# A two-block kernel with a planned instruction order: more places for side work beside the input projections, and an earlier start of four modulation blocks

## The chip, the cores and the metric

The kernel runs on one core of a Trainium2 chip. The metric is the device time of one execution in microseconds; lower is better. The engines are named as the profile names them: PE (matrix multiply, with PEld for its weight loads), DVE (vector), ACT (activation), POOL (GpSimd) and SP (which here only issues DMAs).

## What is computed

The program takes a row matrix `x` of 1024 x 1024 through two blocks, all in float32. What matters of the reference:

```python
# first block
h = rms_norm(x, norm_w)
proj = einsum('bsd,de->bse', h, w_in)            # 1024 -> 6160 columns
gq, gk, gv, glr, hq, hf, hi, xq, gate = split(proj)
# 4 GLA heads and 4 HGRN heads: S_t = diag(g_t) S_{t-1} + k_t v_t^T, o_t = S_t^T q_t
# 4 cross-attention heads over a memory of 256 rows
mixed = concatenate([gla_o, hgrn_o, xo]) * silu(gate)
x = rms_norm(x + einsum('bse,ed->bsd', mixed, w_out), final_norm_w)
# second block
mod = silu(c) @ w_mod + b_mod                    # 6 x 1024: shift, scale, gate, twice
h = modulate(rms_norm_2(x, norm1_g), sh1, s1)
u = h @ w_pw1 + b_pw1; u = a * sigmoid(gate)
u = silu(layer_norm(dwconv(u, w_dw) + b_dw))     # width 31 inside rows of 64
x = x + g1 * (u @ w_pw2 + b_pw2)
x = x + g2 * (square(relu(modulate(rms_norm_2(x, norm2_g), sh2, s2) @ w1)) @ w2)
out = rms_norm_2(x, final_g)
```

## The kernel before, in words

**Products.** Every large product is done as three: each operand is split into a rounded high part and a remainder (`whi`, `wlo` for weights; `hTh`, `hTl` or `acth`, `actl` for activations), and `mm3` (line 444) issues high x high, high x low and low x high into one PSUM tile. Weights arrive by DMA in a tile `wst`; `Weights.plan` (line 278) then lists six pieces of work for it: a cast on ACT into half of `whi`, two subtractions into `wlo` on POOL or DVE, and the same for the other half.

**Main line.** The 1024 rows are worked in two halves of 512. Each half has eight units: four GLA heads (G), two pairs of HGRN heads (H) and two pairs of cross-attention heads (X), in the sequence of the table `ORDER`. Each unit has two to four weight tasks `("in", unit, key)`, the input projections: `in_groups` (line 513) runs them on PE into the PSUM tiles `ps_d`. A group of `cm` (line 495) is 24 matmuls of 512 columns, one of `tm` (line 502) 24 matmuls of 256 or 272 columns. When two units are finished, two output tasks (`out_groups`, line 576) multiply the mixed heads (`mixh`, `mixl`) by `w_out`, eight groups of 12 matmuls of 512 columns. After the second half come `pw1_groups` (line 1100) and `pw2_groups` (line 1202) of the convolution module, which use `tm` too, and then the hidden layer, which the change doesn't touch.

**Side work.** What lies between the projections (factors of the recurrence, scores, masks, states, norms, the modulation) is cut into `Step`s in nine lanes. A step of the recurrence is, for two chunks of 128 rows: `scores` (PE, then COPY_PREDICATED on DVE that puts masked pieces into a tile `at`), `turn` (a transposed key), and `output`, whose first matmul reads `at`. A modulation block (`modulation_steps(cb)`, line 969) loads four tiles `wm` and accumulates them on DVE into `macc`.

**What sets the order.** The kernel has a clock of its own at build time: class `Model` adds up estimated costs per engine, and `M.now` is its time on PE. At each `yield` of a projection group two things happen in the loop at the end of `block_kernel`:

```python
for dt in task.go(hi, lo):
    here += dt
    W.tick(min(1.0, (2.0 if task.key[:2] == ("pw2", 1) else 1.3) * here / task.est))
    service(kind=task.key[0])
```

`W.tick` emits as many of the six weight pieces as the share of the task that is done, times 1.3; `here` grows by 2.6 for each yield and `task.est` is 10.4 for these tasks. `service` emits every step whose inputs are ready by the clock; a step of ordinary rank also needs `room`: DVE's estimated queue must end within the first number of `LIMITS` after `M.now`, ACT's within the second. Each engine then runs its instructions in the order in which they were emitted. `pick` decides which task is staged next: output tasks go ahead of the main line once their two units are finished by the clock. `MODS` says after which unit's gate projection which modulation block may begin; the lane `mod` runs them one after another and then the filter of the convolution.

Of the kernel before, what the change touches and what calls it, by code (L numbers as in the profile page):

```python
# [386 lines left out]
def block_kernel(ctx, tc, x, mem, w_in, w_up, w_kv, w_out, w_mod, w_pw1, w_pw2, w_dw, w_1, w_2,  # L387
# [56 lines left out]
    def mm3(o, pairs, first=True, last=True, more=False):  # L444


        n = len(pairs)
        kw = {"skip_group_check": True} if more else {}
        for i, ((sh, sl), (mh, ml)) in enumerate(pairs):
            PE.matmul(o, sh, mh, start=first and i == 0, stop=False, **kw)  # L450
            PE.matmul(o, sh, ml, start=False, stop=False, **kw)
            PE.matmul(o, sl, mh, start=False, stop=last and i == n - 1, **kw)
# [42 lines left out]
    def cm(p, act, hi, lo, w, c):  # L495

        pairs = [((hi[:, k * w + c:k * w + c + P], lo[:, k * w + c:k * w + c + P]), act.both(k)) for k in range(KT)]
        mm3(p, pairs[:KT // 2], last=False)
        yield TH
        mm3(p, pairs[KT // 2:], first=False)  # L500

    def tm(act, i, hi, lo, w, n):

        p = pt("d")
        c = slice(i * P, (i + 1) * P)
        mm3(p[:, :n], [(act.both(k, c), (hi[:, k * w:k * w + n], lo[:, k * w:k * w + n])) for k in range(KT)])
        return p

    hT = {}
# [3 lines left out]
    def in_groups(t, unit, key, u):  # L513
        kind, h = unit

        def go(hi, lo):
            act = hT[t]
            if key in ("qk", "qf0", "qf1"):
                j = 1 if key == "qf1" else 0
                q = u[f"q{j}"] = s4([P, NT, 192], name="q")  # L520
                p = pt("d")
                yield from cm(p, act, hi, lo, 256, 0)
                A.mul(q[:, :, :P], p.rearrange("p (c t) -> p c t", c=NT), QS if kind == "G" else 1.0)
                yield TH
                k = u[f"k{j}"] = s2([P, T], name="k")
                p = pt("d")
                yield from cm(p, act, hi, lo, 256, P)
                if kind == "G":
                    A.copy(k, p)
                else:  # L530
                    a = u[f"a{j}"] = s2([P, T], name="a")
                    hh = 2 * h + j
                    A.activation(a, p, AF.Sigmoid)
                    A.activation(k, p, AF.Sigmoid, scale=-1.0)
                    V.tensor_scalar(a, a, lbt[:, 4 + hh:5 + hh], lbt[:, 8 + hh:9 + hh], op0=ALU.mult, op1=ALU.add)
                    V.tensor_scalar(k, k, lbt[:, 4 + hh:5 + hh], None, op0=ALU.mult)
                yield TH
            elif key == "v":
                n = 272 if unit == ("G", 3) else 256
                v = u["v"] = s4([P, NT, 256], name="v")  # L540
                g = small(16 * NT, "glr", 1).rearrange("p (i c) -> p i c", i=NT) if n > 256 else None
                for i in range(NT):
                    p = tm(act, i, hi, lo, n, n)
                    if t == 0 and unit == units[0][1] and i < 2:
                        turn0(i + 2)
                    A.copy(v[:, i, :], p[:, :256])
                    if n > 256:
                        V.tensor_copy(g[:, i, :], p[:, 256:272])
                    yield TT
                if n > 256:  # L550
                    gt = glrT[t] = s2([16, T], name="glrT")
                    p = pt("m")
                    for i in range(NT):
                        PE.transpose(p[:16, i * P:(i + 1) * P], g[:, i, :], ident)
                    V.tensor_copy(gt, p[:16, :])
                    mark(("glr", t), gt)
            elif key == "g":
                g = u["gate"] = s4([P, 2, T], name="gate")
                for b in range(2):
                    p = pt("d")  # L560
                    yield from cm(p, act, hi, lo, 256, b * P)
                    A.activation(g[:, b, :], p, AF.Silu)
                    yield TH
            else:
                u["qh"] = s4([P, 2, T], F32R, name="xqh")
                u["ql"] = s4([P, 2, T], F32R, name="xql")
                for b in range(2):
                    p = pt("d")
                    yield from cm(p, act, hi, lo, 256, b * P)
                    A.mul(u["qh"][:, b, :], p, QS)  # L570
                    V.scalar_tensor_tensor(u["ql"][:, b, :], p, QS, u["qh"][:, b, :].bitcast(F32),
                                           op0=ALU.mult, op1=ALU.subtract)
                    yield TH
        return go
# [525 lines left out]
    def pw1_groups(h, cb, part):  # L1100
        def go(hi, lo):
            act = acts[h]
            if part == 0:
                if cb == 0:
                    ys[h] = [s4([P, D], name="y") for _ in range(NT)]
                if (h, cb) == (0, 0):
                    biases(0, 0)
                conv["a", h, cb] = s4([P, NT, 256], name="pa")
            elif (h, cb) != (1, 3):
                biases(*((h, cb + 1) if cb < 3 else (1, 0)))  # L1110
            ba, av = conv["b", h, cb], conv["a", h, cb]
            for i in range(NT):
                p = tm(act, i, hi, lo, 256, 256)
                if part == 0:
                    V.tensor_tensor(av[:, i, :], p[:, :256], ba[:, 0, :], op=ALU.add)
                else:
                    g = s2([P, 2, 256], name="pg")
                    V.tensor_tensor(g[:, 0, :], p[:, :256], ba[:, 1, :], op=ALU.add)
                    A.activation(g[:, 0, :], g[:, 0, :], AF.Sigmoid)
                    V.tensor_tensor(g[:, 1, :], av[:, i, :], g[:, 0, :], op=ALU.mult)  # L1120
                    us = s2([P, 2, 256], F32R, name="us")
                    A.copy(us[:, 0, :], g[:, 1, :])
                    rest(us[:, 1, :], g[:, 1, :], us[:, 0, :].bitcast(F32))
                    later([us], 1, lambda i=i, us=us: conv_fwd(h, cb, i, us))
                yield TT
        return go
# [75 lines left out]
    def pw2_groups(h, nb):  # L1202
        def go(hi, lo):
# [3 lines left out]
            for i in range(NT):  # L1207
                if (h, nb, i) in ((1, 2, 0), (1, 3, 0)):
                    load_w1(nb - 2)
                    done["w1" if nb == 2 else "w1b"] = M.time(raw[nb - 2]) + 2.0  # L1210
                p = tm(acts["v", h], i, hi, lo, 256, 256)
                z = s2([P, 256], name="yg")
                V.tensor_tensor(z, p[:, :256], mods[2][:, c], op=ALU.mult)
                xt = px[h][i]
# [805 lines left out]
GAIN = 0.3  # L2020
FAST = ('kv', 'w1', 'out', 'in', 'pw1', 'pw2', 'w2')
URGENT = (7, 15, 30)
MODS = ((1, 0), (1, 1), (2, 2), (3, 3), (4, 6), (5, 7), (10, 8), (11, 10), (12, 11), (13, 9))
LIMITS = {'in': (3.0, 4.0), '': (3.0, 4.0)}
HOLD = [('in', 6), ('in', 7), ('kv', 0), ('in', 15)]
ORDER = ([('G', 3), ('G', 0), ('G', 2), ('H', 0), ('G', 1), ('H', 1), ('X', 0), ('X', 1)], [('G', 3), ('G', 0), ('G', 1), ('H', 0), ('X', 1), ('H', 1), ('X', 0), ('G', 2)])
N4 = 32
# [63 lines left out]
```

## Time and profile before

| | us |
|---|---|
| median of 3 runs | 2037.58 |
| lowest and highest | 2037.0, 2043.21 |
| the profiled execution | 2028.93 |
| its span, first to last instruction | 2026.8 |
| PE busy | 1945.7 |
| DVE busy | 1512.6 |
| ACT busy | 915.5 |
| POOL busy | 829.7 |

Read it so: the profiled execution is one execution of its own, 8.65 us under the median of the runs; it lies 2.13 us around its span. PE has work in flight in 96% of the span. Since matmuls overlap, an idle stretch of PE shows only where nothing at all is in flight. In the page's forty slices the granted clock of PE is at full speed but for a few, and DMA rises to 70 to 90% only in the last third, the hidden layer.

### The profile page before, as it was taken

The page shows a single profiled execution, that of the slowest core. Times are in us where ns is not written, and L with a number is a line of the kernel's source. Part 1 is how long each engine was busy: PE and PEld are TensorE (multiplying, and loading weights), DVE is VectorE, ACT ScalarE, POOL GpSimd, SP SyncE. Part 2 cuts the span into 40 slices and gives each one's busy share as a digit, 9 for nine tenths or more (in the row PEclk, how much of TensorE's full clock was granted, in tenths as well). Part 3 has the DMA queues.
Part 4 walks back from the last instruction along what each step waited for, and adds up shares of the span by engine and source line. Part 5 has one row for each costly group of instructions (what it writes and reads, how often), then busy time and mean ns, then how long its engine had stood idle before and what let it go on. Part 6 is the DMA issues. An engine that isn't in the chain of part 4 may idle for free.

```text
span 2026.8 us, 29614 instructions
## 1 busy us (share of the span) xinstructions
PE 1945.7 (96%) x10892; PEld 1699.7 (84%) x10892; DVE 1512.6 (75%) x2593; ACT 915.5 (45%) x1790; POOL 829.7 (41%) x752
## 2 busy tenths in 40 slices
PE   8999999999999999998999999999999998899998
PEld 6888898888888888887799999997878886688786
DVE  5688869775677876777757666978888878777876
ACT  6433333455443334344234334235777766443333
POOL 3443443443444432444454343540000003978872
PEclk9999999999999999998999999999999999999999
DMA  5223323241232332322433233241699889877765
GB/s 199 83 104 146 125 105 125 89 162 43 94 145 90 118 124 96 125 84 96 150 122 100 79 98 105 85 151 56 194 299 272 244 262 303 277 271 268 272 248 203
DMA packets 177634, 315.01 MB, mean 155 GB/s; under 512 B 9762, under 2 KB 129442, under 8 KB 163794
## 3 DMA queue, kind: packets, MB, share of 16 engines
q1 hardware_dynamic: 175186, 309.33, 45.3%
q10 hardware_dynamic: 2304, 3.80, 0.5%
q8 instruction: 85, 1.39, 0.3%
q14 instruction: 59, 0.48, 0.1%
HBM read 241.78 MB, written 71.31 MB: 154 GB/s over the span
## 4 chain that ended last, share of the span: by engine, by line
PE 77%; DVE 11%; DMA 4%; ACT 4%; issue 2%; POOL 1%; SPq 0%; DVEq 0%; POOLq 0%; ACTq 0%
PE ps_d L244 50%; PE ps_s L244 20%; PE ps_m L244 7%; DVE macc L244 2%; DMA sl<-so 2%; DVE at L244 2%; DVE zt L244 1%; DVE tw L244 1%; DMA sh<-so 1%; DVE so L244 1%; ACT hc L244 1%; ACT whi L244 1%; POOL tm L244 1%; DVE acc L244 1%; DMA wlo<-sl 0%
## 5 line engine op out<-in xcount | busy, mean ns | idle before, releaser
L244 POOL TENSOR_TENSOR wlo<-wst,whi 128x512 fp32r<-128x512 f32 (+1 forms) x240 | 344.8, 1453 | 376.8 <-ACT whi L244 363.8
L244 PE MATMUL ps_d<-hTh,whi 128*128 128x512 f32 x576 | 232.0, 403 | 0.0
L244 PE MATMUL ps_d<-whi,acth 128*128 128x256 f32 x768 | 221.6, 289 | 7.3 <-DVE yg L244 3.8
L244 ACT CAST whi<-wst 128x1024 fp32r<-128x1024 f32 (+1 forms) x182 | 189.0, 1049 | 81.8 <-PE ps_d L244 72.7
L244 PE MATMUL ps_d<-hTh,wlo 128*128 128x512 f32 x576 | 225.0, 391 | 0.0
L244 PE MATMUL ps_d<-hTl,whi 128*128 128x512 f32 x576 | 224.5, 390 | 0.0
L244 POOL TENSOR_TENSOR wst<-wst,g 128x512 f32<-128x512 f32 x64 | 93.4, 1477 | 316.3 <-DMA g<-g2d 290.9
L244 PE MATMUL ps_d<-whi,actl 128*128 128x256 f32 x768 | 219.9, 286 | 2.1 <-POOL actl L244 1.4
L244 PE MATMUL ps_d<-wlo,acth 128*128 128x256 f32 x768 | 219.3, 285 | 2.3 <-DVE wlo L244 2.3
L244 PE MATMUL ps_s<-tm,whi 128*128 128x512 f32 x620 | 191.8, 391 | 6.1 <-ACT ps_s L244 3.4
L244 PE MATMUL ps_s<-hm,tw 128*128 128x512 f32 x768 | 180.9, 390 | 6.0 <-ACT hc L244 4.6
L244 PEld LDWEIGHTS ps_s<-hm,tw 128*128 128x128 f32 x768 | 143.6, 188 | 37.6 <-ACT hc L244 5.8
L244 PEld LDWEIGHTS ps_d<-whi,acth 128*128 128x128 f32 x768 | 149.2, 194 | 8.3 <-DVE yg L244 4.0
L244 DVE TENSOR_TENSOR wlo<-wst,whi 128x512 fp32r<-128x512 f32 (+1 forms) x128 | 116.7, 922 | 51.6 <-ACT whi L244 50.8
L244 PEld LDWEIGHTS ps_d<-whi,actl 128*128 128x128 f32 x768 | 149.3, 194 | 3.1 <-POOL actl L244 1.9
L244 PEld LDWEIGHTS ps_d<-wlo,acth 128*128 128x128 f32 x768 | 149.3, 194 | 2.8 <-DVE wlo L244 2.5
L244 DVE COPY_PREDICATED at<-msk,ps_s 128x128 f32<-128x128 uint8 (+1 forms) x352 | 117.3, 337 | 41.8 <-PE ps_s L244 27.0
L244 PEld LDWEIGHTS ps_s<-tm,whi 128*128 128x128 f32 x620 | 115.6, 188 | 33.0 <-ACT ps_s L244 5.2
L244 PEld LDWEIGHTS ps_d<-hTh,whi 128*128 128x128 f32 x576 | 108.5, 188 | 23.1 <-issue 2.5
L244 PEld LDWEIGHTS ps_d<-hTh,wlo 128*128 128x128 f32 x576 | 108.1, 188 | 23.4
L244 PEld LDWEIGHTS ps_d<-hTl,whi 128*128 128x128 f32 x576 | 108.5, 188 | 21.0 <-issue 0.2
L244 PE MATMUL ps_s<-tm,wlo 128*128 128x512 f32 x310 | 121.0, 390 | 2.7 <-DMA wlo<-sl 2.7
(289 smaller groups left out, 4977.0 us busy)
## 6 DMA issues: line engine op xcount, KB each, us to landing
wst<-in_w_in_dram SPq DMA_DIRECT2D x46, 1024.0 KB, 4.8
wst<-in_w_dram SPq DMA_DIRECT2D x32, 1024.0 KB, 6.5
sh<-so SPq DMA_DIRECT2D x112, 256.0 KB, 4.3
sl<-so SPq DMA_DIRECT2D x112, 256.0 KB, 4.0
whi<-sh SPq DMA_DIRECT2D x31, 896.0 KB, 4.7
wlo<-sl SPq DMA_DIRECT2D x31, 896.0 KB, 7.3
wm<-in_w_mod_dram SPq DMA_DIRECT2D x48, 512.0 KB, 6.4
wst<-in_w_pw_dram SPq DMA_DIRECT2D x24, 1024.0 KB, 5.0
```

The source lines that it names most:

```text
L244: r = f(*args, **kw)
```

## The change

Three edits. `cm` yields after every two of its eight k-tiles and not after four (three points inside a group and one behind it, before one and one), and `tm` yields once in its middle, where it had no point inside. `MODS` lets the modulation blocks 8, 10, 11 and 9 begin after units 9, 9, 10 and 11, before after 10, 11, 12 and 13 (units are counted from 0, eight to a half). `LIMITS` for the input projections is 4.0 and 5.0, before 3.0 and 4.0.

```diff
     def cm(p, act, hi, lo, w, c):
 
         pairs = [((hi[:, k * w + c:k * w + c + P], lo[:, k * w + c:k * w + c + P]), act.both(k)) for k in range(KT)]
-        mm3(p, pairs[:KT // 2], last=False)
-        yield TH
-        mm3(p, pairs[KT // 2:], first=False)
+        for k in range(0, KT, 2):
+            mm3(p, pairs[k:k + 2], first=k == 0, last=k + 2 == KT)
+            if k + 2 < KT:
+                yield TH
 
     def tm(act, i, hi, lo, w, n):
 
         p = pt("d")
         c = slice(i * P, (i + 1) * P)
-        mm3(p[:, :n], [(act.both(k, c), (hi[:, k * w:k * w + n], lo[:, k * w:k * w + n])) for k in range(KT)])
+        pairs = [(act.both(k, c), (hi[:, k * w:k * w + n], lo[:, k * w:k * w + n])) for k in range(KT)]
+        mm3(p[:, :n], pairs[:KT // 2], last=False)
+        yield TH
+        mm3(p[:, :n], pairs[KT // 2:], first=False)
         return p
...
-                    p = tm(act, i, hi, lo, n, n)
+                    p = yield from tm(act, i, hi, lo, n, n)
...
-MODS = ((1, 0), (1, 1), (2, 2), (3, 3), (4, 6), (5, 7), (10, 8), (11, 10), (12, 11), (13, 9))
-LIMITS = {'in': (3.0, 4.0), '': (3.0, 4.0)}
+MODS = ((1, 0), (1, 1), (2, 2), (3, 3), (4, 6), (5, 7), (9, 8), (9, 10), (10, 11), (11, 9))
+LIMITS = {'in': (4.0, 5.0), '': (3.0, 4.0)}
```

The same `yield from` stands in `pw1_groups` and `pw2_groups`. The number 2.6 that a yield reports (`TH`, `TT`) is as before. No matmul is added or removed: both programs have the same ones, in another order.

**Place 1: SP's queue at the end of the second half.** `wst` are weight loads (`in_w_in` input, `in_w_out` output, `in_w_pw` convolution), `wm` the modulation's, `dft` and `wdw` the filter's, `xn` the rows with which the convolution begins. Before:

```order
L244 DMA wm<-in_w_mod_dram 128x1024 x4
L244 DMA wst<-in_w_in_dram 128x2048 x3
L244 DMA wst<-in_w_pw_dram 128x2048
L244 DMA dft<-in_consts_dram 128x640
L244 DMA wdw<-in_w_dw_dram 31x1024
L244 DMA wst<-in_w_out_dram 128x2x512 x2
L244 DMA xn<-xd_0_71 128x1024
```

Now:

```order
L244 DMA wm<-in_w_mod_dram 128x1024 x4
L244 DMA wst<-in_w_in_dram 128x2048 x4
L244 DMA wst<-in_w_out_dram 128x2x512 x4
L244 DMA dft<-in_consts_dram 128x640
L244 DMA wdw<-in_w_dw_dram 31x1024
L244 DMA wst<-in_w_in_dram 128x2048 x5
L244 DMA wst<-in_w_out_dram 128x2x512 x4
L244 DMA xn<-xd_0_71 128x1024
```

The filter's loads stand some five tasks earlier, and the last pair of output tasks that was staged behind the first convolution weights (`in_w_pw`) is staged ahead of them.

**Place 2: PE at the same seam**, between the last input projection and the first convolution product (`ps_d<-whi,acth`). `ps_s<-q,k` and `ps_s<-Q,K` are scores of the last unit, `ps_s<-ident,xn` and `ps_m<-ident,prob` transposes. Before, without anything left out:

```order
L244 MATMUL ps_m<-wdw,dft 128x512 x2
L244 MATMUL ps_s<-q,k 128x192 x2
L244 MATMUL ps_s<-Q_8564,K_8548 128x192 x2
L244 MATMUL ps_s<-Q_8574,K 128x192 x2
L244 MATMUL ps_s<-Q_8584,K 128x192 x2
L244 MATMUL ps_m<-ident,K 128x128 x2
L244 MATMUL ps_s<-q,k 128x192 x2
L244 MATMUL ps_s<-Q_8564,K_8548 128x192 x2
L244 MATMUL ps_s<-ident,xn 128x128 x12
L244 MATMUL ps_m<-ident,prob 128x128 x4
L244 MATMUL ps_s<-ident,xn 128x128 x16
L244 MATMUL ps_m<-ident,prob 128x128 x4
```

Now, a piece of the same stretch:

```order
L244 MATMUL ps_d<-whi,mixl 128x512
L244 MATMUL ps_s<-Q_8638,K 128x192 x2
L244 MATMUL ps_s<-Q_8648,K 128x192 x2
L244 MATMUL ps_m<-ident,K 128x128 x2
L244 MATMUL ps_s<-q,k 128x192 x2
L244 MATMUL ps_s<-Q_8628,K_8612 128x192 x2
L244 MATMUL ps_s<-ident,xn 128x128 x8
L244 MATMUL ps_d<-whi,mixh 128x512
L244 MATMUL ps_d<-wlo,mixh 128x512
```

The eight output groups of units 12 and 13 (`mixh`, `mixl`, 12 matmuls each) now stand one by one between the scores, transposes and outputs of this stretch; before they stood behind the first convolution task.

**Place 3: PE beside a cm group of the first half**, unit 3, first head (H). `at_122` and `at_123` are the two tiles of masked scores. Before:

```order
L244 MATMUL ps_m<-v,at_122 128x128
L244 MATMUL ps_m<-stH_127,q_2087 128x128
L244 MATMUL ps_m<-v,kT 128x128
L244 MATMUL ps_m<-ident,K 128x128 x2
L244 MATMUL ps_d<-hTh,whi 128x512
L244 MATMUL ps_d<-hTl,whi 128x512
L244 MATMUL ps_d<-hTh,wlo 128x512
L244 MATMUL ps_d<-hTh,whi 128x512
L244 MATMUL ps_d<-hTl,whi 128x512
L244 MATMUL ps_d<-hTh,wlo 128x512
L244 MATMUL ps_d<-hTh,whi 128x512
L244 MATMUL ps_d<-hTl,whi 128x512
```

Now:

```order
L244 MATMUL ps_m<-v,at_122 128x128
L244 MATMUL ps_m<-stH_127,q_1918 128x128
L244 MATMUL ps_m<-v,kT 128x128
L244 MATMUL ps_m<-ident,K 128x128 x2
L244 MATMUL ps_d<-hTh,whi 128x512
L244 MATMUL ps_d<-hTl,whi 128x512
L244 MATMUL ps_d<-hTh,wlo 128x512
L244 MATMUL ps_d<-hTh,whi 128x512
L244 MATMUL ps_d<-hTl,whi 128x512
L244 MATMUL ps_d<-hTh,wlo 128x512
L244 MATMUL ps_m<-v,at_123 128x128
L244 MATMUL ps_m<-stH_127,q_1918 128x128
```

Six projection matmuls stand between the two outputs, before twelve (the piece ends after eight of them).

## Rows read from the trace of the kernel before

**Rows 1.** The page: busy us, share and instructions of each engine; the chain's shares.

```profile
PE 1945.7 (96%) x10892; PEld 1699.7 (84%) x10892; DVE 1512.6 (75%) x2593; ACT 915.5 (45%) x1790; POOL 829.7 (41%) x752
PE 77%; DVE 11%; DMA 4%; ACT 4%; issue 2%; POOL 1%; SPq 0%; DVEq 0%; POOLq 0%; ACTq 0%
```

**Rows 2.** Windows: length, busy us of PE, PEld, DVE, ACT, POOL; clock; DMA.

```profile
50.00:430.00 380.00, 372.01 (x2063) 326.62 (x2062) 298.04 (x575) 146.20 (x291) 165.65 (x152) 1.00 0.33 117
770.00:800.00 30.00, 26.18 (x179) 24.70 (x178) 17.41 (x42) 11.37 (x37) 3.83 (x3) 0.90 0.43 140
935.00:985.00 50.00, 37.46 (x189) 30.99 (x188) 41.10 (x79) 19.05 (x43) 23.02 (x24) 0.83 0.49 155
985.00:1250.00 265.00, 262.68 (x2018) 254.34 (x2017) 167.40 (x273) 101.36 (x160) 115.91 (x110) 1.00 0.28 93
1250.00:1420.00 170.00, 158.99 (x1119) 148.84 (x1119) 138.47 (x217) 68.96 (x108) 66.58 (x62) 0.96 0.29 106
1420.00:2026.00 606.00, 579.23 (x2528) 472.30 (x2526) 478.56 (x692) 338.35 (x625) 235.64 (x184) 1.00 0.80 260
```

**Rows 3.** Chain in order of time: start us, us, what; 512 columns, then 256.

```profile
98.25 2.77 PE ps_d L244 x12
1049.19 2.88 PE ps_d L244 x24
```

**Rows 4.** Timeline of PE at the seam: start us, us, instruction, idle time before it.

```profile
955.87 0.66 PE L244 MATMUL ps_s<-ident,xn 128*128 128x128 f32 x4 [1.15 <-DVE zt L244]
960.97 0.41 PE L244 MATMUL ps_d<-whi,acth 128*128 128x256 f32 x1
967.27 0.39 PE L244 MATMUL ps_d<-whi,acth 128*128 128x256 f32 x1 [1.65 <-ACT acth L244]
974.57 0.28 PE L244 MATMUL ps_d<-whi,acth 128*128 128x256 f32 x1
```

**Rows 5.** Groups of DVE by form: xcount, busy us, mean ns, idle before.

```profile
L244 DVE COPY_PREDICATED at<-msk,ps_s 128x128 f32<-128x128 uint8 x320 | 104.6, 327 | 32.4 <-PE ps_s L244 17.8 <-PE ps_m L244 0.5
L244 DVE TENSOR_TENSOR xl<-ps_d,xl 128x512 f32<-128x512 f32 x64 | 43.8, 685 | 42.3 <-PE ps_d L244 42.0
L244 DVE TENSOR_SCALAR zt<-ps_s,m1s,m1b 128x512 f32<-128x512 f32 x16 | 12.4, 801 | 0.0
```

**Rows 6.** Timelines of DVE and of PE, 785 to 796.

```profile
791.31 1.54 DVE L244 SCALAR_TENSOR_TENSOR macc<-wm,scv,macc 128x512 f32<-128x512 f32 x2 [4.38 <-DMA wm<-in_w_mod_dram]
792.77 2.01 DVE L244 COPY_PREDICATED at<-msk,ps_s 128x128 f32<-128x128 uint8 x6
...
794.92 0.77 PE L244 MATMUL ps_m<-v,at 128*128 128x128 f32 x2 [2.90 <-DVE at L244]
```

**Rows 7.** Waits of PE: us in total, times, longest.

```profile
PE ps_m L244 <- DVE at L244: 11.1, 10, 2.9
PE ps_s L244 <- DVE at L244: 5.1, 9, 1.3
```

**Rows 8.** Timeline of PE in the convolution stage.

```profile
1109.83 0.39 PE L244 MATMUL ps_d<-wlo,acth 128*128 128x256 f32 x1 [2.32 <-DVE wlo L244]
1260.76 0.39 PE L244 MATMUL ps_d<-whi,acth 128*128 128x256 f32 x1 [1.89 <-DVE acth L244]
```

**Rows 9.** Timeline of ACT at the start.

```profile
17.08 2.17 ACT L244 ACTIVATE hTh<-ps_s,pv 128x128 fp32r<-128x128 f32 x8 [2.00 <-PE ps_s L244]
19.34 1.12 ACT L244 CAST whi<-wst 128x1024 fp32r<-128x1024 f32 x1
```

**Rows 10.** Timelines of DVE and POOL, 930 to 936: one form of DVE, alone and beside POOL.

```profile
930.35 0.43 DVE L244 TENSOR_TENSOR Q<-Q,tree 128x256 f32<-128x256 f32 x1
932.84 0.75 DVE L244 TENSOR_TENSOR Q<-q,a 128x256 f32<-128x256 f32 x1
930.70 4.91 POOL L244 TENSOR_TENSOR K<-K,tree 128x256 f32<-128x256 f32 x6
```

More of the change, by code (lines that the diff above doesn't have):

```diff
@@ L1112, in go @@
             for i in range(NT):
-                p = tm(act, i, hi, lo, 256, 256)
+                p = yield from tm(act, i, hi, lo, 256, 256)
                 if part == 0:
@@ L1210, in go @@
                     done["w1" if nb == 2 else "w1b"] = M.time(raw[nb - 2]) + 2.0
-                p = tm(acts["v", h], i, hi, lo, 256, 256)
+                p = yield from tm(acts["v", h], i, hi, lo, 256, 256)
                 z = s2([P, 256], name="yg")
```

## The prediction

> **What bounds the kernel now.** I read the page first. PE is busy in 96% of the span and the chain of waits lies on it for 77%; DVE has 11% of the chain and DMA 4% [rows 1]. So the time is PE's stream, plus what PE waits, plus what it loses at a low clock. The stream cannot shrink: both programs have the same matmuls. The windows then tell where something else than the stream is paid for [rows 2]: 50 to 430, plain projections beside the recurrence, has 7.99 us of PE idle in 380; 985 to 1250, in the convolution, 2.32 in 265; but 935 to 985, the seam between the last input projection and the convolution, has 12.54 idle in 50 and a granted clock of 0.83. The seam's timeline shows both losses [rows 4]: PE waits 1.15 for `zt` on DVE and 1.65 for `acth` on ACT, and between them one matmul of 256 columns takes 0.41, which later takes 0.28: it ran at 1.2 GHz after the idle stretches, and at 2.4 GHz again by 974.57. A second such place, 770 to 800, has 3.82 idle and a clock of 0.90. There DVE waited 4.38 for a `wm` load, the six mask copies behind it took 2.01, and PE stood 2.90 for `at` [rows 6]. The rest are short waits, PE for `at` and for other work of DVE: 11.1 us at ten places and 5.1 at nine [rows 7].
>
> The prices of a gap on PE are twelve matmuls of 512 columns in 2.77 us and 24 of 256 columns in 2.88 [rows 3]: 0.231 and 0.120 each, whatever was issued between them, so cutting a group in two costs nothing by itself.
>
> **The change part by part.**
>
> *The seam.* More points let steps finish earlier by the planner's clock, so the last two output tasks are staged ahead of the convolution, and their eight groups stand between the scores, transposes and outputs (place 2). That is 8 x 2.77 = 22.2 us of PE work put where PE idled. They left the stage 985 to 1250, which is 99% busy and simply becomes shorter. What is to be had is the idle, 12.54, and the low clock, (1 - 0.83) x 37.46 = 6.4: 18.9 in all; the other end is nothing. DVE must keep up: its 41.10 busy us [rows 2] and eight `xl` additions at 0.685 [rows 5] make 46.6, against 37.46 - 6.4 + 22.2 = 53.3 of PE. It fits, with 6.7 to spare. What stays is the two waits at the seam, for `zt` (each 0.801 on DVE [rows 5]) and for `acth` [rows 4], since the convolution still begins with them, 2.8, and the 2% idle of the stage 50 to 430 on 53 us, 1.1. Taken: -18.9 + 3.9 = **-15.0**.
>
> *The modulation.* Blocks 8, 10, 11 and 9 start up to two units sooner, the `wm` loads and the additions into `macc` with them; the filter's loads and its product follow sooner as well. SP gets these loads ahead of weight loads that they stood behind; output weights now stand ahead of convolution weights (place 1). The place at 770 to 800 loses its modulation. Its worth is 3.82 idle and (1 - 0.90) x 26.18 = 2.6 of clock, 6.4; if the blocks meet a late `wm` at their new place and again hold copies up, it costs as much again. DVE's work is the same amount. I take the idle alone, **-4**, between -6.4 and +6.4, because it took a coincidence of a late load and copies right behind it [rows 6] that shows at one block.
>
> *Weight pieces.* `here` grows by 2.6 at each of twice as many yields, so the six pieces of a weight are emitted in the first 40% of a task, not the first 80%. `wlo` comes sooner: the wait of 2.32 for it at 1109.83 [rows 8] can go, **-2** (0 to -2.3). Some ten remainders go from POOL to DVE; at twice the 0.685 of a 512-wide addition [rows 5] that is an estimated 14 us, spread over the run, of a DVE that is busy in 75%. On ACT, 45% busy [rows 1], casts come closer together. Nothing for these; their cover is the idle of both engines, and the third rival is what it costs if that fails.
>
> *Half the spacing, one more microsecond of DVE queue.* This is the edit with a possible loss. Between two steps that follow each other there were twelve projections, 2.77 us, and now often six, 1.39 (place 3). An `output` waits for six copies at 0.327 [rows 5], 2.0 us, in which 2.77 is cover enough and 1.39 is not. But a step is emitted only when its inputs are ready by the clock, so halving offers points and does not force them. Counted over the 32 pairs of scores and first `output` of the second half, 13 had under 3 us of projections between them, and 14 have it now. One pair at the mean wait of 1.1 (11.1 over ten [rows 7]) and as much for the longer queue: **+2**. The ends are -8 (the idle of 50 to 430 goes altogether) and +16 (0.5 us on each of the 32).
>
> *Convolution.* `tm` with a point inside does the same in `pw1` and `pw2`. Between the last transposes of the normalised rows and the product that needs them there were 48 matmuls of 256, now 36: 5.8 against 4.3 us of cover. PE already waited 1.89 for that `acth` [rows 8], so what cover loses the wait gains: **+1.4** (0 to +1.4). From the last `pw2` task on, PE's order is the same, so the 606 us of 1420 to 2026 stay.
>
> *The start.* A CAST of the second weight now precedes a group of turned rows on ACT. It takes 1.12 us, in a place where ACT stood idle for 2.00 [rows 9]. **0** (to +1.1, were that idle gone).
>
> Sum: -15.0 - 4 - 2 + 2 + 1.4 = **-17.6**. The profiled execution took 2028.93 (2026.8 of span and 2.13 around it), so it would take 2011.3. The median of the runs lies 8.65 above that execution; I put the same on top: **2020**.
>
> **The rivals.**
>
> *The waits only move.* The output groups need mixed heads that the same steps produce, and DVE has just 6.7 us to spare in the seam. If they wait for DVE in their turn, the idle of 12.54 comes back among them and only the clock is won. For it: DVE is already what PE waits for there [rows 4]. Against: these groups are 22 us of work that is ready when the two units are. -17.6 + 12.5 = -5.1: 2032 (2028 to 2039).
>
> *Copies under pressure: slower.* If half the spacing, with DVE's limit at 4 and not 3 us, puts the copies of each pair 1 us later than its `output` wants them, 32 pairs pay 32 us. In place of my +2 the sum is -19.6 + 32 = +12.4: 2050 (2040 to 2060). It cancels the gains from 0.61 us a pair. For it: 1.39 us is less than the six copies take. Against: of the whole 2027 us only ten such waits are seen, with a longest of 2.9, though 13 of 32 pairs had under 3 us already.
>
> *DVE and POOL collide.* An operation of DVE on 128x256 takes 0.43 by itself and 0.75 with POOL at work [rows 10]. Pieces of weights that come in a bunch put more of POOL's work, 166 of 380 us, beside DVE's copies. If a tenth more of DVE's 298 us falls beside POOL, that is 30 x 0.74 = 22 us more DVE work out of its 82 idle; PE's 7.99 of idle, grown as that slack shrinks (82/60), becomes 10.9, so +2.9 for each 380 us, and +6.8 over some 880 us of projections: 2027. The Trainium skill, "Perfetto Trace Analysis", section Optimizing Scalar/DVE Operations, says that GpSimd and DVE share a read port of SBUF, so that moving work between the two might not help. By that rule the ten remainders that go to DVE are no loss, and the bunching is; the two durations agree with it, without showing the cause.
>
> *The clock falls in shorter batches.* The stage 50 to 430 had twelve-matmul batches between steps and a clock of 1.00; 1250 to 1420, where more steps lie between, 0.96 [rows 2]. If halved batches brought 0.96 to the projections, 880 us x 0.979 busy x 0.04 = +34: 2054. Against: what stands between the batches is matmuls too, and idle, not switching, went ahead of the low clock at the seam [rows 4]. The Trainium skill, same page, section Matmul Optimizations, says that the engine scales its power by utilisation and wants matmuls back to back in batches. By that rule shorter batches would speak against this change; the seam agrees that idle costs clock, and no row shows a short batch without idle losing any.
>
> *Not as said.* The order's seam could prove empty because the output weights land late (SP has other loads ahead): 2038.
>
> **How the numbers follow.** Chances: forecast 0.53, waits that move 0.20, copies 0.12, collision 0.10, batches 0.03, not as said 0.02. The forecast's own range is 2010 (both places return in full, the other terms at their best ends without the -8) to 2031 (the seam gives half and 770 to 800 nothing). A measurement of this kernel tells about 0.3%, 6.1 us, from no change: faster is under 2031.5, slower over 2043.7. Faster: 0.53, nearly all of the collision (0.09) and 0.06 of the moved waits, 0.68. Slower: batches 0.03 and 0.09 of the copies, 0.12. The rest, 0.20, is no change. The range 2008 to 2041 leaves out most of the copies, the batches, and a few hundredths below.
>
> **What would show it.** Right: the stretch before the convolution has PE over 92% busy at a clock near 1.00, with output groups among scores; no stretch like 770 to 800; PE's waits for `at` near 11 to 15 us; the hidden layer as long as before. Wrong: PE's waits for `at` at 25 us or more, at many places; a clock under 1.00 beside projections with PE busy; mask copies whose mean grows over 327 ns; or output groups that each wait for `mixh` or `mixl`.

## The result: 1.5% faster, by more than was forecast

| | before | after |
|---|---|---|
| median, us | 2039.93 (4 runs, 2037.0 to 2043.21) | 2009.52 (4 runs, 2008.76 to 2012.59) |
| profiled execution, us | 2028.93 | 2009.97 |
| its span, us | 2026.8 | 2007.7 |
| its granted clock, mean | 0.989 | 0.990 |

The ratio is 0.9853, with an interval of 0.9832 to 0.9875. The forecast was 2020 (2008 to 2041): the result lies at the fast end of that range, and just outside the 2010 to 2031 that I gave for the case that my mechanism holds. The two profiled executions differ by 18.96 us, where I had forecast 17.6; the medians differ by 30, and by 28 in a later comparison (e9). The section on why the prediction came out takes both numbers apart.

The page of the changed kernel, engines and chain, answering to [rows 1]:

```profile
PE 1940.9 (97%) x10892; PEld 1693.9 (84%) x10892; DVE 1512.9 (75%) x2603; ACT 918.9 (46%) x1791; POOL 815.1 (41%) x742
PE 79%; DVE 11%; issue 3%; DMA 3%; POOL 2%; ACT 2%; SPq 0%; DVEq 0%; POOLq 0%; ACTq 0%
```

The work is the same and so is each engine's share. PE idles for 2007.7 - 1940.9 = 66.8 us, before 81.1, and its busy time is 4.8 shorter at the same 10892 matmuls. The mean clock of 0.990 for 0.989 makes some 2 us of these 4.8 (0.001 of 1940.9, and three digits are all it is given in); the rest isn't located. The windows show where PE idles. Columns as in [rows 2]; the last one is 606 us of hidden layer, shifted to where it lies now:

```profile
50.00:430.00 380.00, 372.87 (x2053) 326.43 (x2052) 298.86 (x584) 144.90 (x290) 158.31 (x148) 1.00 0.32 114
430.00:770.00 340.00, 333.75 (x1850) 289.85 (x1849) 247.78 (x463) 142.29 (x315) 144.06 (x137) 0.98 0.34 118
770.00:800.00 30.00, 30.00 (x211) 28.51 (x211) 18.52 (x43) 14.66 (x41) 7.51 (x8) 1.00 0.23 71
800.00:935.00 135.00, 134.75 (x749) 116.57 (x748) 94.56 (x201) 61.00 (x160) 59.21 (x65) 1.00 0.24 82
935.00:985.00 50.00, 46.87 (x270) 40.64 (x269) 41.61 (x72) 17.22 (x35) 23.07 (x21) 1.00 0.34 115
985.00:1250.00 265.00, 258.91 (x2046) 252.96 (x2046) 179.59 (x288) 108.55 (x170) 116.53 (x109) 0.99 0.32 112
1250.00:1400.00 150.00, 141.91 (x1004) 131.80 (x1003) 127.20 (x204) 62.42 (x96) 50.88 (x50) 0.99 0.29 104
1401.00:2007.00 606.00, 580.22 (x2509) 472.64 (x2508) 475.35 (x686) 337.77 (x624) 235.20 (x184) 0.99 0.79 259
```

Two windows of the kernel before that [rows 2] doesn't have:

```profile
430.00:770.00 340.00, 335.51 (x1861) 292.22 (x1861) 243.80 (x454) 145.69 (x322) 143.00 (x135) 0.99 0.30 103
800.00:935.00 135.00, 132.61 (x733) 115.15 (x732) 101.14 (x202) 54.52 (x145) 57.93 (x60) 1.00 0.28 98
```

The seam, 935 to 985, has 3.13 us of PE idle where it had 12.54, and a clock of 1.00 where it had 0.83. At 770 to 800 there is no idle at all. From 800 to 935 the idle fell from 2.39 to 0.25, and between 1250 and the hidden layer from 11.01 to 8.09, at a clock of 0.99 and not 0.96. Two windows have become worse: 430 to 770 idles 6.25 (before 4.49, and the clock is 0.98 for 0.99), and the convolution, 985 to 1250, 6.09 (before 2.32, and 0.99 for 1.00). The hidden layer idles 25.78 against 26.77, at 0.99 for 1.00. The windows are stretches of time: after the seam the same work lies some 19 us earlier than before.

PE in the seam, where the last output groups (`mixh`) now stand between scores and transposes:

```profile
945.15 0.89 PE L244 MATMUL ps_s<-q,k 128*128 128x192 f32 x4 [1.57 <-DVE at L244]
948.18 0.33 PE L244 MATMUL ps_s<-ident,xn 128*128 128x128 f32 x1 [0.33 <-DVE xn L244]
949.45 0.48 PE L244 MATMUL ps_d<-whi,mixh 128*128 128x512 f32 x1
952.30 0.59 PE L244 MATMUL ps_m<-v,at 128*128 128x256 f32 x2
```

The longest wait that remains is one of 1.57 for `at`; four more, for `at`, `xn` and `wlo`, are of 0.31 to 0.53. The `output` at 952.30 waits for nothing: twelve matmuls of an output group have run ahead of it. The waits for `zt` and for `acth` that opened the convolution [rows 4] are gone.

Of PE's waits (us in total, times, longest), those that bear on the argument:

```profile
PE ps_d L244 <- DVE pa L244: 5.4, 2, 3.7
PE ps_m L244 <- DVE at L244: 4.8, 6, 1.1
PE ps_d L244 <- DVE yg L244: 4.2, 1, 4.2
PE ps_d L244 <- ACT mixh L244: 3.2, 1, 3.2
PE ps_s L244 <- DVE at L244: 2.4, 3, 1.6
```

The waits for `at` were 11.1 and 5.1 [rows 7] and are 4.8 and 2.4, at nine places and not nineteen. Two kinds of wait are new: `pa`, in the convolution, and `mixh`, early in the second half. The rows of these two, DVE first, then PE:

```profile
1046.94 1.23 DVE L244 TENSOR_TENSOR conv_b_pw<-conv_b_pw,gate_bc 128x1024 f32<-128x1024 f32 x1 [4.79 <-DMA conv_b_pw<-in_rows_dram]
```

```profile
540.84 0.80 PE L244 MATMUL ps_d<-whi,mixh 128*128 128x512 f32 x1 [3.24 <-ACT mixh L244]
1048.55 0.58 PE L244 MATMUL ps_d<-whi,acth 128*128 128x256 f32 x1 [3.75 <-DVE pa L244]
1048.94 0.42 PE L244 MATMUL ps_d<-wlo,acth 128*128 128x256 f32 x1
```

DVE stands 4.79 us for the load of a row, with the additions that read PE's finished tiles (`pa`) queued behind it, and PE waits for them at 1048.55. Behind both waits PE runs at 1.2 GHz: the granted clock is 0.50 from 540.84 to 543.00 and from 1048.55 to 1051.50. The matmul of 512 columns at 540.84 took 0.80, where the first one behind other work takes 0.48 at the high clock (949.45 above); the one of 256 columns at 1048.94 took 0.42, where [rows 4] has 0.28.

### The profile page after: what moved, and what is told of

Same layout as the page of the kernel before. It is cut to its first block, busy times and chain, and to the rows that moved or that the text cites. A ratio compares the mean times of both kernels' runs of the same rounds, so it can differ in the third digit from the quotient of the medians.

```text
span 2007.7 us, 29626 instructions
## 1 busy us (share of the span) xinstructions
PE 1940.9 (97%) x10892; PEld 1693.9 (84%) x10892; DVE 1512.9 (75%) x2603; ACT 918.9 (46%) x1791; POOL 815.1 (41%) x742
## 4 chain that ended last, share of the span: by engine, by line
PE 79%; DVE 11%; issue 3%; DMA 3%; POOL 2%; ACT 2%; SPq 0%; DVEq 0%; POOLq 0%; ACTq 0%
PE ps_d L244 48%; PE ps_s L244 23%; PE ps_m L244 8%; DVE macc L244 2%; DVE at L244 1%; DMA sl<-so 1%; DVE Q L244 1%; POOL tm L244 1%; DVE acc L244 1%; DVE a L244 1%; DVE xn L244 1%; DVE so L244 0%; ACT whi L244 0%; DMA wst<-in_w_in_dram 0%; DVE wlo L244 0%
## 5 line engine op out<-in xcount | busy, mean ns | idle before, releaser
L244 POOL TENSOR_TENSOR wlo<-wst,whi 128x512 fp32r<-128x512 f32 (+1 forms) x232 | 338.9, 1478 | 321.2 <-ACT whi L244 290.8
L244 DVE TENSOR_TENSOR wlo<-wst,whi 128x512 fp32r<-128x512 f32 (+1 forms) x136 | 123.9, 923 | 59.7 <-ACT whi L244 57.3
```

What stands on the lines that cost most here:

```text
L244: r = f(*args, **kw)
```

## The experiments

Theory: the change gains at the seam (idle and clock) and at the modulation; the rest of it is small. Rivals: the finer points gain everywhere; a forced seam only moves the waits; the gain depends on more than these parts. Where a task was moved, it was done by a condition in `pick`, where the planner chooses the next task. The ratios stand against the kernel before, run beside them: 2037.36 us (e1 to e4), 2036.47 (e5 to e8), 2035.22 (e9 to e12).

**e1: the kernel before once more.** No edit.

> The kernel before, unchanged, profiled once more. What is asked: its profiled execution was 8.65 us under the median of its runs and I carried that over to the changed kernel, whose profiled execution lies at its median. Theory A (the first profiled execution was a short one): a new profiled execution takes 2036 to 2041, and the stretches that are longer than in the first profile name 7 to 12 us. Theory B (profiled executions of this kernel are always short): it takes 2027 to 2031 again, and the timed runs of the same kernel lie 8 us above.

Measured: median 2033.94 (2030.77 to 2041.92), ratio 0.9988 (0.9974 to 1.0002); profiled execution 2031.84. So two blocks of runs of the same kernel can lie 0.1 to 0.2% apart, and the profiled execution is again a short one. What goes with it is the granted clock, which each execution reports: the shortest of these twelve had 0.989 and took 2030.77, the longest 0.982 and 2041.92, that is 11.15 us for 0.007, 1.6 us for each 0.001. The clock isn't the whole of the scatter: executions of before at 0.983 took 2034.84 to 2046.31 in the same comparison. The first profiled execution had 0.989 as well; the median of the 23 executions of before in this comparison was 0.984. Neither of the two theories holds as I put it: profiled executions are drawn from a scatter that goes with the clock, and the one I argued from was a good one.

**e2: the seam alone.** The kernel before, and

```diff
         held = main and main[0].key[:2] in HOLD
+        if outs_due and outs_due[0][0] == 12 and main and main[0].key[0] == "pw1":
+            return out_task(*outs_due.pop(0))
```

> The kernel before with one line more in pick: the last two output tasks are staged ahead of the first convolution weight. Points, MODS and LIMITS as before. Theory (the seam is the largest part): 13 to 19 us under before, ratio 0.991 to 0.9935; granted clock near 1.00 between last projection and convolution. Rival (the finer points are what gains, everywhere): within 5 us of before. Rival (waits move): the eight output groups wait for mixh or the copies, 3 to 8 us gained by the clock alone.

Measured: 2032.18, ratio 0.9973 (0.9959 to 0.9987), 5 us and not 13 to 19. The seam did fill. Its window and the convolution's, and PE's rows in both:

```profile
935.00:985.00 50.00, 45.65 (x216) 38.38 (x215) 39.20 (x72) 19.12 (x42) 26.82 (x30) 0.93 0.14 45
985.00:1250.00 265.00, 255.28 (x1999) 247.94 (x1998) 178.64 (x292) 101.27 (x162) 110.01 (x104) 0.99 0.35 114
```

```profile
947.04 0.79 PE L244 MATMUL ps_d<-wlo,mixh 128*128 128x512 f32 x1 [2.09 <-DVE wlo L244]
1049.84 0.67 PE L244 MATMUL ps_m<-macc,ones 128*128 128x512 f32 x1 [2.88 <-DVE macc L244]
1138.19 0.58 PE L244 MATMUL ps_d<-whi,acth 128*128 128x256 f32 x1 [4.10 <-ACT acth L244]
```

The idle in the seam fell from 12.54 to 4.35 us, and that of the convolution rose from 2.32 to 9.72. The remainders of the output weights come late, and the convolution waits for the last modulation (`macc`) and for `acth`. What the seam gives is given back after it: waiting moved, as my rival of moving waits had it, though into another stage. The old `MODS` alone doesn't explain the wait for `macc`: e4 has it too, and no such wait.

**e3: the seam undone in the changed kernel.** In `pick`, the first convolution task is returned ahead of the output tasks of units 12 and 13 (`pw1_seen` is an empty list made just before `pick`).

```diff
+        if outs_due and outs_due[0][0] == 12 and main and main[0].key[0] == "pw1" and not pw1_seen:
+            pw1_seen.append(1)
+            return main.pop(0)
```

> The changed kernel with the last two output tasks held behind the first convolution weight, as they stood before; the rest of the change stays. Theory (seam 15 to 19 us of about 30): 2024 to 2029. Rival (finer points give most): 2010 to 2016.

Measured: 2023.49, ratio 0.993 (0.9911 to 0.9949), 14 us over the changed kernel; the stretch 930 to 985 of this profile:

```profile
930.00:985.00 55.00, 44.44 (x234) 37.30 (x233) 46.93 (x79) 17.52 (x35) 23.57 (x22) 0.88 0.44 142
```

10.56 us of idle and a clock of 0.88 are back, and the time lies just under the theory's 2024 to 2029. Other waits moved with it: that for `yg` is 9.0 us here, in the changed kernel 4.2, and that for `pa`, 5.4 there, is gone. They nearly cancel, so some 14 us are what the filled seam is worth in the changed kernel's order, and 5 in that of before.

**e4: the point in `tm` alone.** The new `tm` and its `yield from` in the kernel before; `cm`, `MODS` and `LIMITS` old.

> Only tm has its new point; cm, MODS and LIMITS as before. By the order of its instructions the eight output groups stand ahead of the convolution here too. Theory: the seam is filled, so 13 to 19 us under before, and the stretch at 770 to 800 (MODS as before) stays as before unless the copies miss the late load: 2018 to 2027. Rival (gain goes with the number of points): a third to a half of the gain at most, spread over the projections, and a seam that still idles: 2028 to 2036.

Measured: 2015.99, ratio 0.9892 (0.9874 to 0.9911). This one edit makes the planner stage the output tasks ahead of the convolution, and gives 21 us, more than I expected of it; the whole change gives 28 beside its own runs of before (e9). Not all of the 21 is the seam:

```profile
50.00:430.00 380.00, 377.11 (x2096) 331.25 (x2095) 297.98 (x577) 149.04 (x294) 166.47 (x152) 1.00 0.33 118
935.00:985.00 50.00, 44.15 (x228) 38.14 (x227) 38.95 (x66) 18.45 (x36) 22.99 (x21) 0.93 0.21 70
```

The seam still idles 5.85 us at a clock of 0.93, and the projections of the first half, 50 to 430, idle 2.89, before 7.99. Both places of the forecast keep a flaw: PE waits 2.92 at 783.09, with DVE late behind a `wm` load, and 5.31 at 944.85 for an output weight's remainder:

```profile
783.09 0.69 PE L244 MATMUL ps_m<-ident,prob 128*128 128x128 f32 x2 [2.92 <-DVE at L244]
944.85 0.79 PE L244 MATMUL ps_d<-wlo,mixh 128*128 128x512 f32 x1 [5.31 <-DVE wlo L244]
```

In the changed kernel the first place has no wait.

**e5: seam, `MODS` and `LIMITS` without any new point.** e2 with the two tables of the change.

> e2's order at the seam with the new MODS and LIMITS, and no new point in cm or tm. Theory (in e2 the filled seam paid its gain back in the convolution, where the late modulation blocks and late output weights made PE wait 2.9 for macc, 4.1 for acth and 4.5 for wlo): with the blocks earlier 8 to 11 of these come back, 2018 to 2026. Rival (the points are what gains, seam and modulation only with them): 2028 to 2034.

Measured: 2033.46, ratio 0.9986 (0.997 to 1.0003): no gain, against my theory and in the range of the rival, that seam and modulation gain only together with the points. The 2.88 for `macc` is gone, as the theory had it (the longest that is left is 1.4), but two other waits came:

```profile
PE ps_d L244 <- ACT mixh L244: 8.5, 1, 8.5
PE ps_m L244 <- DMA wdw<-in_w_dw_dram: 3.6, 1, 3.6
```

**e6: the old `LIMITS` in the changed kernel, seam kept.** `LIMITS` as before and the line of e2.

> The changed kernel with LIMITS as before; without more, the output tasks then stand behind the first convolution weight again, so they are forced ahead of it by one line in pick. Theory (LIMITS only serves to fill the seam): within 4 us of the changed kernel, 2006 to 2014. Rival (the longer DVE queue costs waits for the copies beside projections, 1 us at some pairs): 3 to 8 us faster, 2002 to 2006. Rival (it lets steps through that else wait): 2016 or more.

Measured: 2038.38, ratio 1.0007 (0.9992 to 1.0022). All of the gain is lost, as only my last rival had it, and not to waits for the mask copies (7.7 us, in the changed kernel 7.2): 11.0 for `mixh`, 4.0 for the filter's load, 8.8 for `yg` (4.2 in the changed kernel).

```profile
PE ps_d L244 <- ACT mixh L244: 11.0, 1, 11.0
PE ps_d L244 <- DVE yg L244: 8.8, 2, 8.7
PE ps_m L244 <- DMA wdw<-in_w_dw_dram: 4.0, 1, 4.0
```

After e5 and e6 the theory had to be widened: a small edit moves the planner's whole order, and whether a task is staged just before or just after what it needs is decided anew, with 3 to 11 us at each such place. e10 tests one of them.

**e7: all but `cm`.** The changed kernel with `cm` as before.

> The changed kernel with cm's points as before (one inside a group). Theory (seam and modulation carry the change; the finer points in cm are worth little by themselves): 2007 to 2014, with PE's waits beside the projections within 3 us of the changed kernel's. Rival (cm's points gain everywhere): 2016 to 2022. Rival (they cost, since a copy has half the cover): 2000 to 2006.

Measured: 2023.47, ratio 0.9936 (0.9911 to 0.9961), so `cm`'s points are worth 14 us in this company: against my theory, and slightly more than the first rival. Their loss shows in waits for `yg` (9.2 against 4.2) and for remainders on POOL (5.0 against 1.3):

```profile
PE ps_d L244 <- DVE yg L244: 9.2, 2, 9.0
PE ps_d L244 <- POOL wlo L244: 5.0, 5, 3.9
```

**e8: the row loaded earlier.** In the changed kernel, `bg_step` is split: `bg_load` loads the row, and `bg_step` keeps the product.

```diff
-    lane("mod", [Step(bg_step, ev="bg")])
+    lane("mod", [Step(bg_load), Step(bg_step, lambda: [mods["bg"]], ev="bg")])
```

> The changed kernel with the load of the row conv_b_pw2_2 in a step of its own, and the product with it in a later one, which waits by the planner's clock for the load. In the changed kernel DVE stands 4.8 us for that load at the product, with additions to pa behind it, and PE 3.7 for pa. Theory: the wait goes, 3 to 5 us faster, 2004 to 2007. Rival (the other work of DVE there, the end norm of the rows with its waits for POOL, keeps pa late all the same): within 2 us of the changed kernel.

Measured: 2012.51, ratio 0.9883 (0.9857 to 0.991): no faster than the changed kernel. DVE's wait for the row is gone, and PE's wait for `pa` of 3.75 became 2.52 some 30 us later. The order behind it moved, and in SP's queue the second half's row loads now stand behind four stores and not three; DVE waited for them, and PE for DVE:

```profile
1310.83 5.04 DVE L244 TENSOR_TENSOR xn<-xn,conv_b_pw 128x1024 f32<-128x1024 f32 x4 [8.55 <-DMA xn<-xd]
```

```profile
1316.26 0.58 PE L244 MATMUL ps_d<-whi,acth 128*128 128x256 f32 x1 [8.57 <-DVE yg L244]
```

**e9: the changed kernel once more.** No edit.

> The changed kernel, unchanged, once more, for the scatter of its executions and their granted clock. In the runs so far an execution of the kernel before has a mean clock of 0.979 to 0.989 (median 0.984) and is about 1.5 us longer for each 0.001 less, and its profiled execution was one at 0.989. Theory (the change also takes the places away where the clock falls in most executions): 2008 to 2012 at 0.989 to 0.990, with a spread of under 6 us. Rival (the four executions seen were good ones by chance): 2012 to 2018 at 0.984 to 0.988, spread like that of the kernel before, 10 us or more.

Measured: 2007.62 (2002.2 to 2008.87), ratio 0.9858 (0.9836 to 0.988). The clocks of its executions are 0.991 to 0.993, those of before in the same comparison 0.982 to 0.987 with a median of 0.985. The rival falls; the median is even just under the theory's 2008, and the spread, 6.7 us, just over its 6. Its profiled execution is the 2002.2 one:

```profile
core 0: 2000.0 us, clock 0.993
```

It shows the same waits as the first profile (3.2 for `mixh`, 3.7 for `pa`, 4.4 for `yg`) at a span 7.7 us shorter; 0.003 of clock over 2000 us is 6 of these 7.7.

**e10: the output task of units 6 and 7 held.** The changed kernel, and

```diff
+        if outs_due and outs_due[0] == (6, 0) and main and main[0].key == ("in", 9, "qk"):
+            return main.pop(0)
```

> The changed kernel, with the output task of units 6 and 7 staged behind one more input task, since it is staged before unit 7's mixed head is done and PE waits 3.2 us there for mixh in the changed kernel (8.5 in e5, 11.0 in e6), with a low clock behind it. Theory (such a wait, set by where the planner happens to stage that task, is what e5 and e6 lost): the wait goes, 3 to 6 us faster than the changed kernel, 2003 to 2007. Rival (the order shifts behind it and other waits of the same size come): 2008 to 2016.

Measured: 2000.08 (1998.23 to 2003.09), ratio 0.9826 (0.9805 to 0.9847), 7.5 us under e9 and more than the 3 to 6 expected. The wait for `mixh` is gone from the list, and the stretch in which it lay has 0.05 us of idle at full clock. That stretch here, and 535 to 560 in the changed kernel:

```profile
500.00:560.00 60.00, 59.95 (x310) 51.48 (x309) 40.60 (x89) 26.29 (x75) 25.41 (x26) 1.00 0.21 71
```

```profile
535.00:560.00 25.00, 21.58 (x95) 18.06 (x94) 15.07 (x36) 5.56 (x15) 7.74 (x6) 0.86 0.15 51
```

3.42 of idle and 14% of 21.6 us, 3.0, of low clock: 6.4 of the 7.5. In e9's execution the same stretch has 3.10 of idle and a clock of 0.93, 4.6 in all, so the place accounts for 4.6 to 6.4:

```profile
535.00:560.00 25.00, 21.90 (x98) 18.86 (x99) 12.99 (x33) 5.40 (x15) 6.21 (x5) 0.93 0.13 43
```

**e11: e10, and the second half's rows loaded ahead of the stores.**

```diff
-    put("norm", ln_steps(0) + px_steps(0) + ln_steps(1) + px_steps(1), 20)
+    l1, p1 = ln_steps(1), px_steps(1)
+    put("norm", ln_steps(0) + px_steps(0) + l1[:12] + p1[:1] + l1[12:] + p1[1:], 20)
```

> e10, and the loads of the second half's rows (xn from xd) issued before the last transposes of the convolution's norm, so that they stand ahead of the stores of the first half in SP's queue; in the changed kernel DVE stands 4.7 us for them at the first addition of conv_b_pw, and PE 4.2 behind that for yg (8.6 to 9.0 in e3, e6, e7 and e8). Theory: 3 to 5 us faster than e10, 1999 to 2004. Rival (the loads wait for their buffers and hold the convolution weights behind them): no faster than e10, or up to 5 slower.

Measured: 1999.99 (1997.2 to 2001.02), ratio 0.9823 (0.9803 to 0.9844): as fast as e10, no faster. The loads do leave SP 12 us before the stores,

```profile
1266.06 2.09 SPq L244 DMA_DIRECT2D xn<-xd  x4
1277.73 8.26 SPq L244 DMA_DIRECT2D xd<-xn  x4
```

and PE's waits for `yg` fall from 4.0 to 2.3 (the longest is 1.9); these 2 us are less than the scatter of four or five executions. e10 and e11 are the fastest kernels of this study.

**e12: pieces of weights spread as before.**

```diff
-            here += dt
+            here += dt * (0.5 if task.key[0] in ("in", "pw1", "pw2") else 1.0)
```

> The changed kernel, in which here grows by half as much for each point of in, pw1 and pw2, so that the pieces of a weight are spread over a task as before the change. Theory (the bunching is worth about 2 us by earlier wlo): 2010 to 2016, mask copies with the same mean. Rival (the bunch costs DVE time beside POOL): 3 to 8 us faster, 2002 to 2007, with a lower mean of the mask copies. Third case (the order is sensitive as a whole): here the output task of units 6 and 7 is staged early again, and PE's wait for mixh is 5 to 12 us and not 3, 2016 to 2024.

Measured: 2021.79 (2015.7 to 2025.3), ratio 0.9928 (0.9907 to 0.9948), 14 us over e9. PE's waits for remainders are 11.1 us, in the changed kernel 2.5 (1.3 and 1.2):

```profile
PE ps_d L244 <- POOL wlo L244: 7.7, 8, 3.0
PE ps_d L244 <- DVE wlo L244: 3.4, 2, 3.0
```

The time lies in the range of the third case, but the wait for `mixh` that this case named did not come; one of 4.5 for `prob` stood right ahead of the same output task. The mean of the mask copies (128x128) is 327 ns here, in the changed kernel and before [rows 5]:

```profile
L244 DVE COPY_PREDICATED at<-msk,ps_s 128x128 f32<-128x128 uint8 x320 | 104.8, 327 | 23.8 <-PE ps_s L244 9.2 <-DVE at L244 0.5
```

So the bunch costs the copies nothing, and in this order it is worth about 8.6 us of waits for remainders. They aren't the whole of the 14: the waits for `macc` grew as well, from 2.6 to 9.2, with DVE waiting 11.4 for `wm` loads, in the changed kernel 0.3. In the kernel before, whose pieces were spread in the same way, the waits for remainders were 3.2 us: the same spreading costs little in the old order and much in the new one.

## Why the prediction came out, and where it missed

**Right: what bounds the kernel, and the largest term.** The seam was to give 15.0 us. Its idle fell by 9.4 and its clock loss, 6.4, went: 15.8 by the windows; undoing it cost 14 (e3, with other waits moving too). What I gave as its remainder was wrong in kind: `zt` and `acth` no longer wait, a wait for `at` does. And the seam is not worth this in any order: in e2 most of it went to new waits behind it, 7.4 us of idle in the convolution alone. My sum set each part's gain beside the others as if it stood alone. Nor did I see which edit carries most: the point in `tm` alone gives 21 (e4), while both orders whose seam was filled by force without it give 5 and 3 (e2, e5; the 3 isn't clear of the scatter). That this point is enough in any company is not so: e6 has it, and gains nothing.

**Right in direction, too small: the modulation, -4.** I took the 3.82 of idle and left the 2.6 of clock out. The window 770 to 800 gave both, 6.4, the end of my range; the blocks met no such late load at their new place. DVE's waits for `wm`, before and now:

```profile
DVE macc L244 <- DMA wm<-in_w_mod_dram: 7.0, 4, 4.4
DVE macc L244 <- DMA wm<-in_w_mod_dram: 0.3, 1, 0.3
```

In e4, with the old table, the place keeps its wait of 2.92. The 2.6 of clock is a matter of the execution: at the same place the kernel before has 0.96 in e1, and e2, with the old table, 0.99.

**Too small: the pieces of weights, -2.** I priced the one wait for `wlo` that the profile showed, and PE's waits for remainders did fall only from 3.2 to 2.5 us. But without the early pieces the new order has 11.1 (e12): what they are worth could not be read from waits of the old order.

**Wrong in sign: half the spacing, +2.** The step that failed is the price set on "One pair at the mean wait of 1.1" and on the longer queue. I had looked for 11 to 15 us of waits for `at`; they fell from 16.2 to 7.2. 3.7 of these 9 belong to the place at 770 to 800, and the seam keeps as much as it had, 2.4. So the rival of the copies under pressure falls. But it isn't the shorter spacing that did this alone: e7, with `cm` as before, has 6.6 us of such waits, and e5, with no new point at all, 6.4. The orders of before and of e2 (14.4) have many, e4 has 9.4, and all others 4.2 to 7.7; what sets this wasn't isolated. Cover counted between a score and its `output` said nothing about it.

**Missed: two new waits.** `mixh`, 3.2 and its low clock, 6.4 together, and `pa`, 5.4 and some low clock behind it. My rival of moving waits looked for them among the output groups of the seam; the first lies 400 us ahead of it, at the output task of units 6 and 7, the second in the convolution, where I had counted only cover of the transposes. The +1.4 there did not come: the wait of 1.89 for `acth` at the first product of `pw2` [rows 8] is gone from the list.

**As forecast: the start, 0.** The changed kernel idles 9.4 us in its first 50, before 9.0, and in e9 8.7. Its clock there is 0.97 and not 1.00, worth 1.2 us, but that isn't the change: e2, whose PE, DVE and ACT run the same instructions there in the same order as before, has 0.97 too.

**Not quite free: the cut.** I put 0.231 us on a matmul of 512 columns "whatever was issued between them". Behind scores or transposes the first one of an output group takes 0.48 to 0.53 and the second starts 0.31 to 0.37 later, so each switch costs some 0.1 us. The busy time of PE, 4.8 shorter, shows no sum of it.

**Wrong: the 8.65 us on top.** This is most of the distance from 2020 to 2009.5. Between the two profiled executions my -17.6 met -18.96. But the profiled execution of before ran at a mean clock of 0.989, and the median of its executions is 0.984 or 0.985: at 1.6 us for 0.001 that is 6 to 8 us, about the offset. The four executions of before in the result were also long ones: their median is 2039.93, in the later comparisons 2035.22 to 2037.36. The profiled execution of the changed kernel had 0.990 and its runs 0.989 to 0.993, so there is no such offset behind it. The difference in clock between the medians goes with a part of the gain, and I had carried it over as if it belonged to the measurement. That fewer idle stretches are why fewer executions fall to the low clock is what the windows suggest, and no run isolates it. In which places the slower executions of before lose their clock isn't shown: both profiles of it are from the faster part of the scatter.

**Luck: that -17.6 met -18.96.** The seam and 770 to 800 gave 22.2 us by the windows, where I had 19.0; so the rest of the kernel gave 3.1 back, where my other terms make 1.4. But that rest is not made of my terms. Its idle is a sum of +1.8 (430 to 770), +3.8 (the convolution) and +0.4 (the start), against -2.1 (800 to 935), -2.9 (behind the convolution), -0.9 and -1.0 (50 to 430 and the hidden layer). And 9.0 of the 22.2 are clock, of which only some 2 remain over the whole execution: the clock fell nearly as much, in other places. A second pair of profiled executions, those of e1 and e9, differs by 29.6.

**The other rivals.** A clock that falls in shorter batches: beside the projections it is 1.00 as before (50 to 430), so no; the 0.98 of 430 to 770 holds the wait for `mixh`. DVE against POOL: the copies' mean is unchanged, DVE is busy 298.86 us from 50 to 430 where this rival had 22 more than 298.04, and the bunch that it feared saves waits (e12), so no. Moved waits: in the changed kernel they are 8.6 us, `pa` and `mixh`, and most of the gain stays; in e2, e5 and e6 waits of this kind took most or all of the gain.

What was not tried: e6 with the output task of e10 held, which would show how much of its 28 us that one wait carries. And the old `MODS` with all new points, and the new `MODS` in the kernel before without `LIMITS`, have no run, so `MODS` alone has no price.

## What to carry to other kernels

Where a planner decides the order, an edit has no price of its own: the same filled seam gave 5 us in one order and 14 in another, and most new orders here brought one or two misplaced tasks of 3 to 11 us that the list of waits names at once. So look through that list after each edit and try to mend its longest new line before judging the edit. One of the three mended here paid (e10: 7.5 us for two lines); e8 took its wait away and e11 shortened its own, and neither gained anything that can be told from the scatter; in e8 the order behind it moved and another wait grew. Before carrying an offset between one profiled execution and the median over to another kernel, compare the granted clock of that execution with the clocks of the others.

## What the hardware showed that was not expected

The same program, with the same waits, took 2000.0 or 2007.7 us of span at mean clocks of 0.993 and 0.990 (e9 and the first profile), and the kernel before 2030.77 to 2041.92 at 0.989 to 0.982. A short wait can cost as much again behind it, and not in every execution: 3.4 us of idle in the 25 us around 541 went with 3.0 us of low clock in the first profile, and 3.1 with 1.5 in e9. The place where the clock falls isn't a property of the order alone: e2 has the instructions of before in its first 50 us, and 0.97 there where before has 1.00.
